# Gating and summing the output projection's weights: from the gate stages to a background task of the projection stream

## The chip, the cores and the metric

The kernel runs on one core of a Trainium2 chip. The metric is device time in microseconds (us) of one execution; lower is better. The core's engines are PE (TensorE, matrix products), DVE (VectorE), ACT (ScalarE), POOL (GpSimd) and SP (SyncE, which here only issues DMA loads). Each engine works through its own list of instructions in order, and waits where an instruction needs something that another engine or a DMA has not delivered.

## The reference, cut to what matters

One layer of a trunk whose two mixers (HGRN2 and GLA) share one input projection; sequence length and width are both 1024, everything is float32.

```python
mod = c_act @ ada_w + ada_b
shift, scale, gate = jnp.split(mod, 3, axis=-1)
h = rms_norm(x, norm_w) * (1.0 + scale) + shift
hq, hf, hi, hz, gq, gk, gv, gz, ga, mg = jnp.split(h @ w_in, IN_OFFSETS, axis=-1)
y_h = hgrn2_branch(hq, hf, hi, hz, ...)
y_g = gla_branch(gq, gk, gv, gz, ga, ...)
u_h, u_g = y_h @ w_branch[0], y_g @ w_branch[1]
mg = sigmoid(mg.reshape(B, T, 2, D_MODEL))
merged = mg[:, :, 0] * u_h + mg[:, :, 1] * u_g
x = x + gate[:, None, :] * (merged @ w_out)
return rms_norm(x, final_norm_w)
```

The factor `gate` scales columns, so `gate * (merged @ w_out)` is `merged @ (w_out * gate)`. The kernel multiplies the weights by the gate once. That multiplication, and the sums of blocks of the result, are what the change moves.

## The kernel before, in words

Every large product is done in float32 accuracy by splitting each operand into a rounded part `hi` (a cast on ACT, line L196 or L1285) and the rest `lo` (a subtraction on DVE, L197 or L1286), and by three PE products of the parts. On the time axis of the profile the kernel has these parts:

* The start (to about 75 us): modulation vectors, norm of the input, transposes.
* **The projection stream** (to about 806 us). Class `Stream` holds a list of jobs, one per block of columns of `w_in`; each job loads its weights (`load_feat`, L523, on SP), splits them and runs its PE products (L541). After each unit of a job, `weave` (L895) lets two tracks go on: `side`, which holds the attention of the heads (scores L683 to L781, outputs L848 and L850, squares and writes of the results through L1095, L1107 and L916), and `back`, a first-in first-out queue of background tasks. `back` holds first `prepare()` (factors of h and sums of other weights, `weight_sums`), and then `gate_side()`, which is appended when the first HGRN value block is done and makes the tile `gate_b`, the gate broadcast over the partitions (about 616 to 646 us).
* **Four seven-product stages** (`last_stages`): two gate stages b=0 (about 806 to 893 us) and b=1 (to about 975), which project the merge gates, and two branch stages b=2, 3 (to about 1130). Each is a two-by-two block product by seven products p in the order 1, 2, 5, 3, 6, 7, 4, with four pairs i of output tiles each. `Pair.run` holds the PE products (L1343); a pair's accumulator is turned into gates by ACT (L1414) and written to DRAM by POOL (L1415). Inputs are loaded ahead: factors by `fetch_factor` (L1230) and split by `build` (ACT L1263, DVE L1264, for p = 3 ACT L1260, DVE L1261), weights by `load_duo` (sums of weights L1274, plain ones L1278) and split by `prep_duo` (ACT L1285, DVE L1286). ACT copies of accumulators by `seed` and `snap_of` are L1323 and L1315.
* The output stage b=4 (1130 to 1210 us), again seven products, with the weights that the change is about: they are loaded back from DRAM by `load_w4` and split.

The first products of stage b=0 begin before the attention of the last head (h = 7) is done, so from about 795 to 860 us the last attention and the first gate products run interleaved. The bank of PSUM that the stage uses is lent to it when the last projection blocks have been read (`L953` on DVE multiplies the last one out of PSUM) and when the scores are done.

**The weights of the output projection** are four blocks for each of kk = 0, 1. In before, `load_wy(kk)` loads four 512 KB tiles (L1466, SP), `gate_wy` multiplies each by `gate_b` (L1474, DVE), `sum_wy` forms four sums of them (L1484, DVE), and `keep_wy` writes seven results per kk to DRAM (L1469, on POOL's queue, destination `wo`). These steps hang on hooks of the gate stages: `after(b, p, i, f)` puts f behind pair i of product p of stage b. For kk = 0 the load is at (0, 3, 0), the gating at (0, 6), the sums at (0, 7), and the tiles are freed at (1, 1, 0); for kk = 1 they are at (1, 1, 2), (1, 5), (1, 6) and (1, 7, 3). The multiplications and sums are held at that place of DVE's list by `tc.keep_in_program_order`; other instructions of an engine may be put in another order by a scheduler, by when it reckons their inputs and buffers to be ready.

All tiles of 4 KB per partition come from one pool `S`. A new tile takes the place of an older one, and whatever writes it must wait until the last reader of the older one is done; that reader can be a DMA write.

Of the kernel before, what the change touches and what calls it, by code (L numbers as in the profile page):

```python
# [9 lines left out]
F32 = mybir.dt.float32  # L10
# [5 lines left out]
P = 128  # L16
D = 1024
T = 1024
# [13 lines left out]
OUT_PRODUCTS = (1, 5, 3, 6, 7, 2, 4)  # L32
# [51 lines left out]
def hybrid_trunk_kernel(  # L84
# [6 lines left out]
    nc = tc.nc  # L91
# [5 lines left out]
    dp = ctx.enter_context(tc.tile_pool(name="dram", bufs=1, space=bass.MemoryType.DRAM))  # L97
# [3 lines left out]
    S = Slots(sp, N_SLOTS)  # L101
# [806 lines left out]
    stream = Stream()  # L908
# [5 lines left out]
    def put_act(acts, d, y):  # L914
        for half in range(2):
            nc.gpsimd.dma_start(acts[half][d // 2][:, d % 2 * 512:d % 2 * 512 + 512], y[:, half * 512:half * 512 + 512])  # L916
        S.free(y)
# [92 lines left out]
    def start_side(gen, wait=1):  # L1010
        stream.side.append([gen, wait])
# [30 lines left out]
    gate_b = [None]  # L1042

    def gate_side():

        gacc, gbias = S.get([D]), S.get([D])
        nc.sync.dma_start(gbias[0:1, :], ada_b[0:1, 2 * D:3 * D])
        for k in range(KT):
            b = S.get([D])
            nc.sync.dma_start(b, ada_w[0, k * P:(k + 1) * P, 2 * D:3 * D])  # L1050
            if k == 0:
                nc.vector.tensor_scalar_mul(gacc, b, cs[:, 0:1])
            else:
# [32 lines left out]
    def hgrn_attention(h):  # L1086
        st = h_state
        y = [None]
        sq = [None]

        def post(vh, half, po):
            if half == 0:
                y[0], sq[0] = st.pop(("z", h)), S.get([T])
            sl = slice(half * 512, half * 512 + 512)
            nc.scalar.activation(sq[0][:, sl], po, AF.Square)  # L1095
            nc.vector.scalar_tensor_tensor(y[0][:, sl], po, vec[:, R_HN + h:R_HN + h + 1],
                                           y[0][:, sl], ALU.mult, ALU.mult)

        yield from attention(st.pop(("q", h)), st.pop(("k", h)), st.pop(("f", h)), lambda: st[("v", h // 4)],
                             h % 4 * P, P, post, 4 if h % 4 == 1 else 3)  # L1100
        if h % 4 == 3:
            S.free(*st.pop(("v", h // 4)))
        put_act(yh_d, h, y[0])
        if ssq[0] is None:
            ssq[0] = sq[0]
        else:
            nc.gpsimd.tensor_add(ssq[0], ssq[0], sq[0])  # L1107
            S.free(sq[0])
        if h == 7:
            yield 2  # L1110
            rst = S.get([T])
            yield from inverse_root(rst, ssq[0], D)
            S.free(ssq[0])
            rst_h[0] = rst

    def hgrn_v(h):
        def done(v):
            h_state[("v", h // 4)] = v
            if h == 0:
# [59 lines left out]
    sources += [[branch(n, d) for d in range(0, 8, 2)] for n in (1, 0)]  # L1179

    w_sums = [[[dp.tile([P, T], F32, name=f"ws{b}{j}{i}") for i in range(4)] for j in range(2)] for b in range(4)]

    def weight_sums(b, i):
# [22 lines left out]
    def prepare():  # L1206
        yield from factors(h_d, f_x)
        for b in range(4):
            for i in range(4):
                yield from weight_sums(b, i)  # L1210

    stream.back.append([prepare(), 60])


# [4 lines left out]
    X_OF = {1: (0, 0), 2: (1, 0), 4: (1, 1)}  # L1219
# [50 lines left out]
    def load_duo(b, p, j):  # L1270
# [4 lines left out]
        else:  # L1275
            kh, f = X_OF[p]
            for a in range(2):
# [29 lines left out]
    class Pair:  # L1307
# [42 lines left out]
        def after(self, p):  # L1350
            bank, snap, out = self.bank, self.snap, outs[self.b]
            if p == 1:
                if self.b:
                    self.seed()
                else:
                    snap[1] = self.snap_of("a", -1.0)
            elif p == 2:
                out(2 * self.i, 0, bank["a"], False)
                R.free(bank.pop("a"))
            elif p == 5:  # L1360
                snap[5] = self.snap_of("e")
# [88 lines left out]
    for g in BUILT[1:]:  # L1450
        n = GROUPS.index(g)
# [3 lines left out]
    for d in range(8):  # L1455
        after(*((2, 5) if d % 2 else (1, 4)), d // 2, lambda d=d: load_gate1(d))

    w4_d = {p: [dp.tile([P, T], F32, name=f"wo{p}{kk}") for kk in range(2)] for p in OUT_PRODUCTS}
    w_rows = w_out[0].rearrange("(i two p) c -> two p i c", two=2, p=P)
    wy, w4_raw, W4 = {}, {}, {}  # L1460

    def load_wy(kk):
        for kh in range(2):
            for f in range(2):
                t = wy[kh, f] = S.get([2, 512])
                nc.sync.dma_start(t, w_rows[kh][:, 2 * kk:2 * kk + 2, f * 512:f * 512 + 512])  # L1466

    def keep_wy(p, kk, kh, f):
        nc.gpsimd.dma_start(w4_d[p][kk], wy[kh, f].rearrange("p a f -> p (a f)"))  # L1469

    def gate_wy(kk, n):
        kh, f = ((0, 0), (0, 1), (1, 0), (1, 1))[n]
        t = wy[kh, f]
        tc.keep_in_program_order(nc.vector.tensor_mul(  # L1474
            t, t, gate_b[0][:, f * 512:f * 512 + 512].unsqueeze(1).to_broadcast([P, 2, 512])))
        for p, at_ in X_OF.items():
            if at_ == (kh, f):
                keep_wy(p, kk, kh, f)
        if kk == 1 and n == 3:
            S.free(gate_b[0])  # L1480

    def sum_wy(kk, n):
        p, dst, other = ((7, (0, 0), (0, 1)), (5, (0, 1), (1, 1)), (6, (1, 1), (0, 0)), (3, (1, 0), (1, 1)))[n]
        tc.keep_in_program_order(nc.vector.tensor_add(wy[dst], wy[dst], wy[other]))  # L1484
        keep_wy(p, kk, *dst)

    def drop_wy():
        S.free(*wy.values())
        wy.clear()

    def load_w4(p):
        w4_raw[p] = [S.get([2, 512]) for _ in range(2)]
# [84 lines left out]
    def out_stage():  # L1577
        for p in OUT_PRODUCTS:
# [6 lines left out]
                S.free(*z)  # L1585
            for z in W4.pop(p):
                S.free(*z)

    for kk, (lead, first, then) in enumerate((((0, 3, 0), (0, 6), (0, 7)), ((1, 1, 2), (1, 5), (1, 6)))):
        after(*lead, lambda kk=kk: load_wy(kk))  # L1590
        after(*((1, 1, 0) if kk == 0 else (1, 7, 3)), drop_wy)
        for n in range(4):
            after(*first, n, lambda kk=kk, n=n: gate_wy(kk, n))
            after(*then, n, lambda kk=kk, n=n: sum_wy(kk, n))

    def last_of_11():
        combine(4, "22", "22", "11")
# [121 lines left out]
```

## Time and profile before

| what | value |
|---|---|
| time before, median of 3 runs | 1215.93 us (1215.64 to 1216.92) |
| the profiled execution's own time | 1216.46 us |
| its span in the profile | 1214.8 us |
| granted PE clock | 0.998 of full speed |
| busy: PE, DVE, ACT, POOL | 1184.1, 790.9, 546.9, 123.8 us |
| PE not busy within the span | 30.7 us |
| the operations that the change moves: DVE L1474 and L1484 | 8 x 1.22 us each |
| their loads (SP, L1466) and writes (POOL, L1469) | 8 and 14 of 512 KB |

A row of the timeline gives the start, the time an instruction (or a run of like ones) took, the engine, the line, the operation, "out<-in" by the names of tiles, the shapes, the count, and in brackets how long the engine sat idle just before and what ended that. Tile names without their number read `b` (pool tiles), `pd`, `pm`, `sc_ps` (PSUM). In the groups by line the columns behind the bar are busy time, mean ns of one, and idle time before. A row by windows gives the stretch, its length, the busy time of each engine with its count of instructions, the granted clock, the busy share of the DMA engines and the data rate.

### The profile page before, as it was taken

Reading aid. Unit: us, or ns where it says so; the run is one execution under the profiler, and the core shown is the slowest. Engines: PE = TensorE matmul, PEld = TensorE weight load, DVE = VectorE, ACT = ScalarE, POOL = GpSimd, SP = SyncE. Lnnn points to the kernel's source line nnn. Section 1 sums busy time; section 2 is a strip of 40 time slices with the busy share of each in tenths; the row PEclk is TensorE's granted clock in tenths of the full one; section 3 lists DMA queues with packets and bytes.
Section 4 is the critical chain, followed back from the end, with each engine's and each line's share of the span. In section 5 each row is a group of like instructions: output and inputs, shape, how many; then the busy total and the mean of one; then the engine's idle time right before and its main releaser. Section 6 shows DMA issues by size and latency. Waiting matters only on the chain.

```text
span 1214.8 us, 20860 instructions
## 1 busy us (share of the span) xinstructions
PE 1184.1 (97%) x8579; PEld 982.6 (81%) x8579; DVE 790.9 (65%) x1245; ACT 546.9 (45%) x797; POOL 123.8 (10%) x215
## 2 busy tenths in 40 slices
PE   5999999999999999999999999999999999999997
PEld 3777889889798888888887888877778888878886
DVE  4637444774848456877884365794653775988994
ACT  5646732434434244344332324455743544444554
POOL 4100000202111121121110101011220000000000
PEclk9999999999999999999999999999999999999999
DMA  9814000844444267255341112054697746435523
GB/s 320 277 70 139 18 19 19 293 141 161 156 152 149 66 207 249 94 179 169 108 174 47 59 53 70 36 174 158 227 343 277 260 160 208 135 104 173 174 104 122
DMA packets 130961, 183.51 MB, mean 151 GB/s; under 512 B 7467, under 2 KB 97633, under 8 KB 130866
## 3 DMA queue, kind: packets, MB, share of 16 engines
q1 hardware_dynamic: 117250, 136.87, 35.7%
q0 software_dynamic: 13568, 45.31, 9.6%
q8 instruction: 67, 1.10, 0.4%
q14 instruction: 28, 0.23, 0.1%
q10 hardware_dynamic: 48, 0.01, 0.0%
HBM read 132.87 MB, written 49.28 MB: 150 GB/s over the span
## 4 chain that ended last, share of the span: by engine, by line
PE 61%; issue 23%; DVE 3%; ACT 3%; POOL 2%; DMA 1%; POOLq 0%; ACTq 0%; DVEq 0%
PE pd L541 19%; PE pd L1343 9%; PE sc_ps L1343 5%; PE pm L1343 5%; PE pd L1520 3%; PE pd L643 2%; PE pd L644 2%; PE pd L645 2%; PE sc_ps L1520 2%; PE pm L848 1%; PE pd L352 1%; PE pm L829 1%; PE pm L850 1%; PE pm L1520 1%; PE sc_ps L352 1%
## 5 line engine op out<-in xcount | busy, mean ns | idle before, releaser
L541 PE MATMUL pd<-b,b 128*128 128x512 f32 x1632 | 387.4, 394 | 0.0
L541 PEld LDWEIGHTS pd<-b,b 128*128 128x128 f32 x1632 | 302.4, 188 | 64.8 <-issue 1.4
L1343 PE MATMUL pd<-b,b 128*128 128x512 f32 x720 | 173.7, 392 | 4.3 <-ACT b L1414 2.1
L1343 PEld LDWEIGHTS pd<-b,b 128*128 128x128 f32 x720 | 133.7, 188 | 35.7 <-ACT b L1414 3.2
L197 DVE TENSOR_TENSOR b<-b,b 128x1024 fp32r<-128x1024 f32 (+2 forms) x89 | 98.9, 1122 | 83.1 <-ACT b L196 65.4
L196 ACT CAST b<-b 128x1024 fp32r<-128x1024 f32 (+2 forms) x89 | 82.9, 948 | 92.1 <-DVE b L1199 14.6
L1286 DVE TENSOR_TENSOR b<-b,b 128x1024 fp32r<-128x1024 f32 x56 | 68.3, 1224 | 66.9 <-ACT b L1285 52.3
L1285 ACT CAST b<-b 128x1024 fp32r<-128x1024 f32 x56 | 58.3, 1050 | 73.9 <-PE pd L1343 20.6
L1343 PE MATMUL sc_ps<-b,b 128*128 128x512 f32 x324 | 79.4, 391 | 1.0 <-ACT scT L793 1.0
L600 PE MATMUL pd<-b,b 128*128 128x256 f32 x256 | 74.2, 290 | 0.0
L1264 DVE TENSOR_TENSOR b<-b,b 128x1024 fp32r<-128x1024 f32 x48 | 59.2, 1251 | 20.8 <-ACT b L1263 15.1
L602 PE MATMUL pd<-b,b 128*128 128x256 f32 x256 | 72.5, 283 | 0.0
L601 PE MATMUL pd<-b,b 128*128 128x256 f32 x256 | 72.4, 283 | 0.0
L1343 PEld LDWEIGHTS sc_ps<-b,b 128*128 128x128 f32 x324 | 60.3, 188 | 14.6 <-ACT scT L793 1.4
L1343 PE MATMUL pm<-b,b 128*128 128x512 f32 x300 | 72.1, 389 | 0.0
L1263 ACT CAST b<-b 128x1024 fp32r<-128x1024 f32 x48 | 49.9, 1050 | 41.2 <-PE pd L1343 16.0
L1343 PEld LDWEIGHTS pm<-b,b 128*128 128x128 f32 x300 | 56.3, 188 | 11.7
L352 PE MATMUL pd<-b,b 128*128 128x512 f32 x192 | 53.3, 410 | 2.0 <-ACT b L196 0.9
L1201 POOL DMA_DIRECT2D ws<-b x64 | 34.6, 541 | 192.0 <-DVE b L1195 86.5
L735 ACT COPY xb<-b 128x512 f32<-128x512 f32 x48 | 29.4, 620 | 49.4 <-PE sc_ps L715 26.7
L643 PE MATMUL pd<-b,b 128*128 128x512 f32 x128 | 51.3, 401 | 0.0
L644 PE MATMUL pd<-b,b 128*128 128x512 f32 x128 | 50.0, 390 | 0.0
(285 smaller groups left out, 1964.3 us busy)
## 6 DMA issues: line engine op xcount, KB each, us to landing
b<-in_w_in_dram SPq DMA_DIRECT2D x66, 512.0 KB, 4.2
ws<-b POOLq DMA_DIRECT2D x64, 256.0 KB, 3.3
b<-ws SPq DMA_DIRECT2D x32, 512.0 KB, 4.9
b<-in_x_dram SPq DMA_DIRECT2D x16, 512.0 KB, 5.7
b<-in_ada_w_dram SPq DMA_DIRECT2D x32, 256.0 KB, 6.9
b<-in_w_branch_dram SPq DMA_DIRECT2D x16, 512.0 KB, 4.4
b<-h SPq DMA_DIRECT2D x14, 512.0 KB, 4.3
wo<-b POOLq DMA_DIRECT2D x14, 512.0 KB, 5.7
```

Of the source, the lines that this page charges most:

```text
L196: nc.scalar.copy(hi, src)
L197: nc.vector.tensor_sub(lo, src, hi.bitcast(F32))
L352: nc.tensor.matmul(accs[f], wg(a, d, f), b[d][:, half * 512:half * 512 + 512], start=(d == 0 and n == 0), stop=(d == KT - 1 and n == 2))
L541: nc.tensor.matmul(ps[0:w, th * 512:(th + 1) * 512], a[:, k, 0:w], b[:, th * 512:(th + 1) * 512], start=(k == 0 and n == 0), stop=(k == KT ...
L600: nc.tensor.matmul(o, lh, hi[:, k % 4, :], start=(k == 0), stop=False)
L601: nc.tensor.matmul(o, lh, lo[:, k % 4, :], start=False, stop=False)
L602: nc.tensor.matmul(o, ll, hi[:, k % 4, :], start=False, stop=(k == KT - 1))
L643: nc.tensor.matmul(o, lh, hi[:, k % 2, :], start=(k == 0), stop=False)
L644: nc.tensor.matmul(o, lh, lo[:, k % 2, :], start=False, stop=False)
L1286: nc.vector.tensor_sub(lo, t, hi.bitcast(F32))
L1343: nc.tensor.matmul(o, a[:, sl], c, start=(p in (1, 5) and kt == 0 and n == 0), stop=(kt == 3 and n == 2), skip_group_check=True)
L1520: nc.tensor.matmul(o, a, b, start=(p in (1, 5) and kt == 0 and n == 0), stop=(kt == 3 and n == 2), skip_group_check=True)
```

## The change

The four steps leave the hooks and become a generator `out_weights()`, appended to the queue `back` right behind `gate_side()`. It waits until 12 tiles are free, loads one kk, gates the four tiles, sums them, frees them, and does the same for the other kk. `drop_wy` is folded in, the two `tc.keep_in_program_order` are dropped, and some names are defined earlier. `load_wy`, `keep_wy`, `gate_wy` and `sum_wy` are otherwise unchanged. In after, the load is line L1222, the write L1225, the gating L1230, the sum L1239, and the lines of before behind them are moved down by 45 (`fetch_factor` is L1275, `load_duo` L1319 and L1323, `prep_duo` L1330 and L1331, `build` L1305 to L1309, the ACT copy of `snap_of` L1360).

```diff
             h_state[("v", h // 4)] = v
             if h == 0:
                 stream.back.append([gate_side(), 4])
+                stream.back.append([out_weights(), 4])
...
+    def gate_wy(kk, n):
+        kh, f = ((0, 0), (0, 1), (1, 0), (1, 1))[n]
+        t = wy[kh, f]
+        nc.vector.tensor_mul(t, t, gate_b[0][:, f * 512:f * 512 + 512].unsqueeze(1).to_broadcast([P, 2, 512]))
...
+    def out_weights():
+        for kk in range(2):
+            while len(S.free_list) < 12:
+                yield 1
+            load_wy(kk)
+            yield 8
+            for n in range(4):
+                gate_wy(kk, n)
+                yield 2
+            yield 4
+            for n in range(4):
+                sum_wy(kk, n)
+                yield 3
+            S.free(*wy.values())
+            wy.clear()
...
-        tc.keep_in_program_order(nc.vector.tensor_mul(
-            t, t, gate_b[0][:, f * 512:f * 512 + 512].unsqueeze(1).to_broadcast([P, 2, 512])))
...
-        tc.keep_in_program_order(nc.vector.tensor_add(wy[dst], wy[dst], wy[other]))
...
-    for kk, (lead, first, then) in enumerate((((0, 3, 0), (0, 6), (0, 7)), ((1, 1, 2), (1, 5), (1, 6)))):
-        after(*lead, lambda kk=kk: load_wy(kk))
-        after(*((1, 1, 0) if kk == 0 else (1, 7, 3)), drop_wy)
-        for n in range(4):
-            after(*first, n, lambda kk=kk, n=n: gate_wy(kk, n))
-            after(*then, n, lambda kk=kk, n=n: sum_wy(kk, n))
```

The number of instructions on each engine stays the same. All 16 multiplications and sums, all 8 loads and all 14 writes now stand in the lists between the jobs of the projection stream that ran from about 640 to 715 us in before. Three places of the lists matter below.

SP's list where the stream loads the weights of its last jobs (L523, from `w_in`), before. `h_116` to `h_119` are the first factors of the gate stage, `b_6828` receives the weights of the job that runs at about 718 us:

```order
L523 DMA b_6233<-in_w_in_dram 128x8x128
L523 DMA b_6390<-in_w_in_dram 128x8x128
L523 DMA b_6828<-in_w_in_dram 128x8x128
L523 DMA b_6473<-in_w_in_dram 128x8x128
L523 DMA b_6535<-in_w_in_dram 128x8x128
L523 DMA b_6645<-in_w_in_dram 128x8x128
```

SP's list at the same job in after, where those weights go into `b_6859`:

```order
L1222 DMA b_6677<-in_w_out_dram 128x2x512
L1222 DMA b_6679<-in_w_out_dram 128x2x512
L1222 DMA b_6683<-in_w_out_dram 128x2x512
L1222 DMA b_6681<-in_w_out_dram 128x2x512
L1275 DMA b_7220<-h_116 128x1024
L1275 DMA b_7446<-h_118 128x1024
L523 DMA b_6859<-in_w_in_dram 128x8x128
L1275 DMA b_7447<-h_119 128x1024
```

The load stood third among the stream's loads and now stands behind the four loads of kk = 1 and two loads of factors. The tile `b_7446` ahead of it takes the place of the tile `b_6679`, so that its load waits for the write of `b_6679` to DRAM (`wo_772<-b_6679` in POOL's list).

DVE's list from the masks of the last head's scores to the operation (L720) behind which its last score products wait, before:

```order
L953 TENSOR_TENSOR b_7437<-b_7437,pd_7336 128x1024
L690 TENSOR_TENSOR blk<-sc_ps,eye_679 128x256
...
L698 COPY_PREDICATED blk<-mask_683,sc_ps 128x64
L1286 TENSOR_TENSOR b_7529<-b_7408,b_7528 128x1024
L717 TENSOR_TENSOR b_7164<-xb,tot_726 128x64x12
L718 TENSOR_TENSOR tot_726<-tot_726 128x64
L719 TENSOR_TENSOR tot_726<-tot_726 128x64
L721 TENSOR_TENSOR tot_726<-tot_726 128x64
L746 TENSOR_TENSOR tot_726<-tot_726 128x32
...
L720 TENSOR_TENSOR b_7330<-b_7330,tot_726 128x64x12
```

The same stretch of DVE's list in after:

```order
L953 TENSOR_TENSOR b_7483<-b_7483,pd_7382 128x1024
L1309 TENSOR_TENSOR b_7689<-b_7649,b_7687 128x1024
L690 TENSOR_TENSOR blk<-sc_ps,eye_679 128x256
...
L698 COPY_PREDICATED blk<-mask_683,sc_ps 128x64
L717 TENSOR_TENSOR b_7210<-xb,tot_726 128x64x12
L718 TENSOR_TENSOR tot_726<-tot_726 128x64
L1331 TENSOR_TENSOR b_7781<-b_7578,b_7780 128x1024
L719 TENSOR_TENSOR tot_726<-tot_726 128x64
L1306 SCALAR_TENSOR_TENSOR b_7871<-b_7801,b_7869 128x1024
L721 TENSOR_TENSOR tot_726<-tot_726 128x64
L1331 TENSOR_TENSOR b_7850<-b_7670,b_7849 128x1024
L720 TENSOR_TENSOR b_7376<-b_7376,tot_726 128x64x12
```

Between L953 and L720 stood one operation of 128x1024 that belongs to the gate stage (L1286), and now there are four (L1309, L1331, L1306, L1331); rows that are the same on both sides (L695 to L711, two more L746) are left out here. The three L746 moved behind L720.

ACT's list at about 850 us, where the last head's outputs are squared (L1095), the accumulators copied (L1315, in after L1360) and the sum of squares cast (L196), before:

```order
L1095 ACTIVATE b_7845<-pm_7848 128x512
L1315 COPY b_7821<-sc_ps 128x512
L1263 CAST b_7940<-b_7889 128x1024
L1315 COPY b_7887<-pd_7440 128x512
L196 CAST b_7906<-b_4458 128x1024
```

And in after:

```order
L1095 ACTIVATE b_7891<-pm_7894 128x512
L1330 CAST b_8010<-b_7916 128x1024
L1360 COPY b_7867<-sc_ps 128x512
L196 CAST b_7952<-b_4458 128x1024
L1308 CAST b_7986<-b_7935 128x1024
L1360 COPY b_7933<-pd_7486 128x512
```

The copy out of `pd` stood ahead of the cast L196, which reads the sum that POOL makes (L1107), and now stands behind it.

More of the change, by code (lines that the diff above doesn't have):

```diff
@@ L1179, in hybrid_trunk_kernel @@
     sources += [[branch(n, d) for d in range(0, 8, 2)] for n in (1, 0)]
+    X_OF = {1: (0, 0), 2: (1, 0), 4: (1, 1)}
     w_sums = [[[dp.tile([P, T], F32, name=f"ws{b}{j}{i}") for i in range(4)] for j in range(2)] for b in range(4)]
@@ L1210, in prepare, with load_wy, keep_wy, sum_wy @@
                 yield from weight_sums(b, i)
+    w4_d = {p: [dp.tile([P, T], F32, name=f"wo{p}{kk}") for kk in range(2)] for p in OUT_PRODUCTS}
+    w_rows = w_out[0].rearrange("(i two p) c -> two p i c", two=2, p=P)
+    wy = {}
+    def load_wy(kk):
+        for kh in range(2):
+            for f in range(2):
+                t = wy[kh, f] = S.get([2, 512])
+                nc.sync.dma_start(t, w_rows[kh][:, 2 * kk:2 * kk + 2, f * 512:f * 512 + 512])
+    def keep_wy(p, kk, kh, f):
+        nc.gpsimd.dma_start(w4_d[p][kk], wy[kh, f].rearrange("p a f -> p (a f)"))
+    def gate_wy(kk, n):
+        kh, f = ((0, 0), (0, 1), (1, 0), (1, 1))[n]
+        t = wy[kh, f]
+        nc.vector.tensor_mul(t, t, gate_b[0][:, f * 512:f * 512 + 512].unsqueeze(1).to_broadcast([P, 2, 512]))
+        for p, at_ in X_OF.items():
+            if at_ == (kh, f):
+                keep_wy(p, kk, kh, f)
+        if kk == 1 and n == 3:
+            S.free(gate_b[0])
+    def sum_wy(kk, n):
+        p, dst, other = ((7, (0, 0), (0, 1)), (5, (0, 1), (1, 1)), (6, (1, 1), (0, 0)), (3, (1, 0), (1, 1)))[n]
+        nc.vector.tensor_add(wy[dst], wy[dst], wy[other])
+        keep_wy(p, kk, *dst)
+    def out_weights():
[13 more added lines that the diff above has]
+            wy.clear()
     stream.back.append([prepare(), 60])
@@ L1218, in hybrid_trunk_kernel @@
     BUILT = [g for g in GROUPS if g[0] != 1]
-    X_OF = {1: (0, 0), 2: (1, 0), 4: (1, 1)}
     BANK = {1: "a", 2: "a", 5: "e", 3: "e", 6: "b", 7: "b", 4: "b"}
@@ L1456, in hybrid_trunk_kernel @@
         after(*((2, 5) if d % 2 else (1, 4)), d // 2, lambda d=d: load_gate1(d))
[L1458 to L1474, printed above, removed]
-            t, t, gate_b[0][:, f * 512:f * 512 + 512].unsqueeze(1).to_broadcast([P, 2, 512])))
[L1476 to L1483, printed above, removed]
-        tc.keep_in_program_order(nc.vector.tensor_add(wy[dst], wy[dst], wy[other]))
[L1485 to L1489, printed above, removed]
+    w4_raw, W4 = {}, {}
     def load_w4(p):
```

## The prediction

> **What bounds the kernel now.** I read the windows first, then PE's waits, then the timeline around each wait. The windows give the busy time of each engine in the parts that the change touches, PE, PE's weight loads, DVE, ACT and POOL from the left.
>
> ```profile
> 640.00:720.00 80.00, 80.00 (x648) 64.12 (x647) 32.73 (x60) 24.80 (x38) 3.44 (x3) 1.00 0.18 50
> 795.00:860.00 65.00, 61.99 (x521) 49.88 (x521) 45.41 (x70) 36.41 (x56) 9.53 (x10) 1.00 0.58 199
> 860.00:900.00 40.00, 38.18 (x167) 31.05 (x168) 26.41 (x27) 24.47 (x32) 9.68 (x18) 1.00 0.76 265
> 900.00:970.00 70.00, 70.00 (x310) 57.98 (x309) 35.56 (x34) 31.63 (x43) 4.27 (x8) 1.00 0.83 279
> ```
>
> PE is never idle where the work goes to (640 to 720 us), nor in the second gate stage, which it leaves (900 to 970), although the DMAs are busy there for 0.83 of the time. It is idle for 3.01 us between 795 and 860 and for 1.82 us between 860 and 900. What the change can win lies in these 4.8 us; what it can lose is open. PE's waits name them:
>
> ```profile
> PE pd L1343 <- ACT b L1414: 2.1, 2, 1.8
> PE pd L1343 <- DVE b L953: 1.5, 1, 1.5
> PE sc_ps L1343 <- ACT scT L793: 1.0, 1, 1.0
> PE pd L1343 <- ACT b L1315: 0.2, 1, 0.2
> ```
>
> So 10 us of moved DVE work in each gate stage is not 10 us on the path: the path is PE, and PE waits at five places there, for 4.7 us.
>
> **The moved work itself.** Of 30 moved instructions the sixteen on DVE cost
>
> ```profile
> L1474 DVE TENSOR_TENSOR b<-b,b 128x1024 f32<-128x1024 f32 x8 | 9.7, 1220 | 0.5 <-DMA b<-in_w_out_dram 0.5
> ```
>
> for the gating, and the sums, of the same shape, as much: 8 x 1.22 = 9.8 us for each kk. These rows show where they can go:
>
> ```profile
> 645.19 1.23 DVE L197 TENSOR_TENSOR b<-b,b 128x1024 fp32r<-128x1024 f32 x1 [6.22 <-ACT b L196]
> 655.77 0.69 DVE L710 TENSOR_TENSOR xb<-b,tot 128x512 f32<-128x512 f32 x1 [9.35 <-PE sc_ps L683]
> 700.02 1.22 DVE L953 TENSOR_TENSOR b<-b,pd 128x1024 f32<-128x1024 f32 x1 [1.48 <-ACT b L952]
> 709.84 1.03 ACT L1077 ACTIVATE b<-pd 128x1024 f32<-128x1024 f32 x1 [7.51 <-PE pd L541]
> 710.90 0.82 DVE L1079 TENSOR_SCALAR b<-b,oml,lb 128x1024 f32<-128x1024 f32 x1 [9.66 <-ACT b L1077]
> ```
>
> The kk = 0 half fills the 9.35 us of idle time ahead of 655.77, the kk = 1 half the 9.66 us ahead of 710.90. Some of it overhangs by a microsecond; the weights that the stream splits there (L197) are read 20 us later. L953, which empties a PSUM bank, moves from 700 to about 705 us behind the last gating; PE takes that bank for its next job about 709.8 us, when the job ahead is done and ACT starts to read it (709.84). **I take 0** for this work; without that cover it would be 10 us per half.
>
> **Term a, SP's queue.** The moved list puts a load that PE needs behind a load that waits for a write. Its rows are the load, the split of what it brings, and the product that needs DVE's list up to L679:
>
> ```profile
> 646.45 0.37 SPq L523 DMA_DIRECT2D b<-in_w_in_dram  x1
> 694.76 0.55 POOL L916 DMA_DIRECT2D yh<-b  x1
> 711.67 1.05 ACT L196 CAST b<-b 128x1024 fp32r<-128x1024 f32 x1
> 715.57 1.21 DVE L197 TENSOR_TENSOR b<-b,b 128x1024 fp32r<-128x1024 f32 x1
> 716.70 0.64 DVE L679 TENSOR_TENSOR xb<-xb,b 128x256 f32<-128x256 f32 x1
> 717.89 1.31 PE L683 MATMUL sc_ps<-xb,b 128*32 128x80 f32 x64
> ```
>
> In before the load went out at 646.45 and had 61 us to spare. In after it stands behind `b_7446<-h_118`, which waits until `b_6679` is gated (row at about 702 to 705 us, since the fourth load can go out only when the write of 694.76 has left its tile, about 697), summed (about 706 to 708) and written. How long writes and loads of 512 KB take, from issue to landing, first for `wo` in the crowded gate stage, then for POOL's writes of `h` at a quiet time, then for the stream's loads from 636 to 740 us:
>
> ```profile
> DMA to landing us min/median/max: 4.0/5.7/7.6
> DMA to landing us min/median/max: 2.9/3.1/6.6
> DMA to landing us min/median/max: 3.7/3.8/3.8
> ```
>
> The DMAs are busy 0.18 here, so I take the quiet rows: write out at 707, landed at 710.3 (709.6 to 713), the load out at 710.8, landed at 714.8 (713.6 to 717.3). ACT's cast (1.05) brings it to 715.9, against the 715.57 at which L197 could start; L679 then ends at 717.7 and PE, which comes free at 717.9, loses little. **I take +0.4** (0 to +3.4; the upper end with 5.5 us for the write and 5 for the load).
>
> The Trainium skill, page "DMA: Bandwidth & Descriptors", section "Anatomy of one DMA — SWDGE (gpsimd) path", fits such a DMA by 2.0 us plus the bytes over 436 GB/s, an estimate of 3.2 us for 512 KB; no row of `wo` here comes below 4.0. By it this term would be about 0.
>
> **Term b, the crossover at 810 to 836 us.**
>
> ```profile
> 809.48 1.23 DVE L1264 TENSOR_TENSOR b<-b,b 128x1024 fp32r<-128x1024 f32 x1
> 810.62 1.23 DVE L953 TENSOR_TENSOR b<-b,pd 128x1024 f32<-128x1024 f32 x1
> 811.90 5.73 PE L1343 MATMUL pd<-b,b 128*128 128x512 f32 x24 [1.49 <-DVE b L953]
> 817.93 0.60 DVE L746 TENSOR_TENSOR tot<-tot 128x32 f32<-128x32 f32 x3
> 818.52 0.96 DVE L720 TENSOR_TENSOR b<-b,tot 128x768 f32<-128x768 f32 x1
> 822.62 0.19 DVE L759 COPY_PREDICATED blk<-mask,sc_ps 128x32 f32<-128x32 int32 x1
> 824.04 0.63 PE L770 MATMUL sc_ps<-xb 128*16 128x16 f32 x56
> 834.02 1.89 PE L1343 MATMUL sc_ps<-b,b 128*128 128x512 f32 x7 [0.96 <-ACT scT L793]
> ```
>
> DVE starts one operation right behind the other in these rows, so what the scheduler puts ahead is paid in full. Ahead of L953 stand the same six splits as before, but in other places, and beside the addition that POOL makes for each head (L1107). What such a meeting costs DVE shows one head earlier:
>
> ```profile
> 752.00 2.40 POOL L1107 TENSOR_TENSOR b<-b,b 128x1024 f32<-128x1024 f32 x1 [0.31 <-ACT b L1095]
> 753.27 2.21 DVE L197 TENSOR_TENSOR b<-b,b 128x1024 fp32r<-128x1024 f32 x1 [0.63 <-ACT b L196]
> ```
>
> L197 takes 2.21 there and 1.21 in the row at 715.57: 1.0 more. I allow L953 that +1.0 (-0.5 to +2.2: a meeting that before had goes, or a second comes).
>
> The Trainium skill, page "SBUF — State Buffer", section "Who interferes with whom", says that a DVE instruction with two inputs in SBUF contends with a GpSimd instruction that reads SBUF, and that whoever issues first keeps the shared pair while the other is blocked for the whole instruction. The row agrees that DVE is held, but for 1.0 and not for all of POOL's 2.40; a full block of a split that starts right behind POOL would make L953 some 2.4 late, and the sum 1.4 higher.
>
> Behind L953 three more operations of 128x1024 come before L720. They start about 1.14 us apart (809.48 and 810.62), so 3 x 1.14 = 3.4, less 0.6 for the three L746 that move behind L720. L759 ends 1.2 us before PE's L770 (822.81 and 824.04): 2.8 - 1.2 = 1.6 that PE would lose, and 2.6 with the delay of L953. The operations that went ahead are gone from the stretch behind, where DVE's way to L793 gets shorter, so the waits of 0.96 and of 0.3 (the L1414 row's 2.1 less its longest), together 1.2, should go: 2.6 - 1.2 = **+1.4** (-0.5 to +3.2).
>
> **Term c, ACT at 850 us.**
>
> ```profile
> 850.46 0.58 ACT L1315 COPY b<-pd 128x512 f32<-128x512 f32 x1
> 852.22 1.05 ACT L196 CAST b<-b 128x1024 fp32r<-128x1024 f32 x1 [1.18 <-POOL b L1107]
> 859.83 2.56 PE L1343 MATMUL pd<-b,b 128*128 128x512 f32 x10 [0.15 <-ACT b L1315]
> ```
>
> The copy out of `pd` ended at 851.04 and now comes behind a cast that waits for POOL until 852.2. Behind it stand further casts and the second copy, for which PE waits at 859.83. A delay of about 1.35 there, less what is slack, gives **+1.2** (0 to +2.1).
>
> **Term d, the end of stage b = 0.**
>
> ```profile
> 887.31 0.54 POOL L1415 DMA_DIRECT2D gate<-b  x1 [3.01 <-ACT b L1414]
> 887.84 0.54 POOL L1469 DMA_DIRECT2D wo<-b  x1
> 892.22 0.60 ACT L1414 ACTIVATE b<-pd 128x512 f32<-128x512 f32 x1 [0.76 <-DMA gate<-b]
> 892.87 1.43 PE L1343 MATMUL pd<-b,b 128*128 128x512 f32 x5 [1.82 <-ACT b L1414]
> ```
>
> PE waits 1.82 for a gate, which waits 0.76 for a tile that the write of 887.31 holds; seven writes of `wo` share queue and DMAs with it, and the casts ahead on ACT wait for loads in the same crowd. With those gone most of it goes: **-1.5** (-1.8 to 0). Stage b = 1 gives nothing, since PE has no idle time there.
>
> **Sum:** 0 + 0.4 + 1.4 + 1.2 - 1.5 = +1.5. The profiled execution took 1216.46, so 1218.0; it lies 0.53 above the median of the runs, so the median comes to **1217.4**.
>
> **The rivals.** A measurement of this kernel can tell about 0.2% from no change, 2.4 us: below 1213.5 is faster, above 1218.4 slower.
>
> *Slower: SP's queue at full price.* If the weights of `b_6859` land after about 715.2, all that is later is paid at L683. For: the fourth load waits for the write of 694.76, and `wo` writes took 5.7 in the middle. Against: the DMAs are quiet. With +2.9 in place of 0.4 the median is 1219.9.
>
> *Faster: the crossover costs nothing.* If the splits that move ahead fill waits of DVE (for data that comes later in after), b and c are 0 and only d is left, at its full 1.8: 1216.46 - 1.8 - 0.53 = 1214.1. For: as many operations stand ahead of L953 as before. Against: none of the DVE rows from 809 to 823 shows idle time ahead of it. It would be below 1213.5 only if the 1.49 at 811.9 went too (1212.6).
>
> *The change doesn't do what it says in the gate stage.* If PE's 1.82 at 892.87 come from the casts of weights (L1285) ahead on ACT and not from the crowd, d is 0: 1218.9.
>
> **How the numbers follow.** Forecast 0.46, of which a quarter lies above 1218.4; slower rival 0.26; faster 0.18, of which a third lies below 1213.5; no change in the gate stage 0.10. Faster is then 0.06 and some for what I overlook, 0.08; slower 0.11 + 0.24 + 0.07 = 0.42; the rest, 0.50, within 0.2%. The range leaves out the ends: from 1213.9 (the faster rival with a little over) to 1221.5 (the slower rival with the upper half of b).
>
> **What would show it.** In the profile after: no idle PE from 640 to 715 us; the start of L683 near 717.9 to 718.3 (term a, 720 or more for the slower rival); PE's idle time ahead of L770 at 824 (b, 1 to 3 us); the wait for L1315's line at 860 (c, over 1 us); and no wait of 1.8 us at 893 (d). The forecast is wrong if the stream shows a wait that these rows don't name, above all of PE for weights, or if DVE at the crossover is idle.

## The result, and the profile after

The changed kernel takes 1224.37 us (median of 6 runs, 1221.40 to 1226.50), against 1215.93 for the kernel before (6 runs, 1215.64 to 1217.28): a ratio of 1.0067, with a 95% interval from 1.0051 to 1.0082. Run again later beside other kernels it took 1222.08 (6 runs), a ratio of 1.0050 (1.0035 to 1.0064). It is slower by 6 to 8 us, where 1.5 was forecast, and it lies above the range. The profiled execution took 1225.01 us (span 1223.1).

The windows of the changed kernel, with the columns as in the prediction:

```profile
640.00:720.00 80.00, 77.44 (x622) 62.57 (x625) 49.32 (x74) 23.44 (x36) 10.92 (x17) 0.99 0.56 185
795.00:860.00 65.00, 57.93 (x510) 46.74 (x509) 47.83 (x72) 34.26 (x54) 9.11 (x10) 1.00 0.51 170
860.00:900.00 40.00, 38.01 (x167) 30.76 (x165) 17.71 (x19) 25.63 (x32) 3.78 (x7) 1.00 0.49 153
```

The moved work is where it was expected: DVE is busy for 49 us instead of 33 between 640 and 720, and the gate stages have lost it. But PE is now idle for 2.56 us in the stream, for 7.1 instead of 3.0 between 795 and 860, and still for 2.0 between 860 and 900. Its waits after 600 us name the places:

```profile
PE pd L1388 <- DVE b L953: 3.3, 1, 3.3
PE sc_ps L683 <- DVE xb L679: 2.6, 1, 2.6
PE sc_ps L1388 <- ACT scT L793: 1.3, 1, 1.3
PE pd L1388 <- ACT b L1360: 1.2, 1, 1.2
PE pd L1388 <- ACT b L1459: 1.1, 2, 0.8
PE pd L1388 <- DVE b L1375: 1.1, 1, 1.1
PE pd L1388 <- ACT b L1362: 0.9, 1, 0.9
PE sc_ps L770 <- DVE blk L759: 0.6, 1, 0.6
```

How far the same PE product (counted in order within its line) lies behind its time in before gives the price of each place. This execution ran 1.73 us ahead in the stream, up to 719 us; 1.6 us of that lead is there from the stream's first products on, far ahead of the moved work:

| product | start before | start after | shift | what lies between |
|---|---|---|---|---|
| L541, up to 719 us | 517.59 | 515.86 | -1.73 | |
| first gate product (L1343, L1388) | 806.06 | 808.57 | +2.51 | wait at L683 and slow clock, +4.24 |
| L1343 after the crossover | 847.35 | 853.46 | +6.11 | waits for L953, L759, L743, L793, +3.60 |
| behind ACT's copy at 850 | 859.83 | 866.75 | +6.93 | wait for L1360, +0.8 |
| at 880 | 880.00 | 889.14 | +9.14 | waits for L1362 and L1375, +2.2 |
| end of stage 0 | 892.87 | 901.15 | +8.28 | wait for L1459 smaller than L1414's was, -0.9 |
| output stage (L1520, in after L1534) | 1130.35 | 1138.61 | +8.26 | nothing |

**The wait at L683.** SP's, POOL's, DVE's and PE's rows around 715 us, then the windows of that stretch:

```profile
708.55 0.34 SPq L1275 DMA_DIRECT2D b<-h  x1
708.98 0.54 SPq L523 DMA_DIRECT2D b<-in_w_in_dram  x1
```

```profile
704.38 0.53 POOL L1225 DMA_DIRECT2D wo<-b  x1 [2.87 <-DVE b L1239]
```

```profile
716.87 1.23 DVE L197 TENSOR_TENSOR b<-b,b 128x1024 fp32r<-128x1024 f32 x1 [2.96 <-ACT b L196]
718.01 0.63 DVE L679 TENSOR_TENSOR xb<-xb,b 128x256 f32<-128x256 f32 x1
```

```profile
718.79 2.07 PE L683 MATMUL sc_ps<-xb,b 128*32 128x80 f32 x64 [2.56 <-DVE xb L679]
```

```profile
713.00:716.00 3.00, 3.00 (x15) 2.34 (x13) 0.91 (x2) 0.21 (x1) 0.00 (x0) 1.00 0.92 267
716.00:719.00 3.00, 0.44 (x15) 0.24 (x17) 2.13 (x3) 0.84 (x1) 0.00 (x0) 1.00 0.29 117
719.00:722.50 3.50, 3.50 (x68) 2.99 (x60) 3.36 (x7) 0.93 (x2) 0.00 (x0) 0.52 0.00 0
```

The chain is the one of term a: the write of 704.38 lands, the factor load of 708.55 may go, and the weights go out right behind it at 708.98. They went out when I had reckoned (710.8, less the 1.7 us by which this execution runs ahead), but took longer: DVE's split waits for the cast, of 1.05 us, until 716.87, so that the weights landed about 715.8, nearly 7 us after their issue and not 4 (in the second profile, shown below, the cast starts 6.2 us after the issue). The DMAs are busy at 0.92 here, not at 0.18. Then comes what no term had: from 719.0 to 722.5 the granted clock is 0.52, so that 3.5 us of products do the work of 1.8. The wait of 2.56 costs 4.24 in all.

**The crossover.** DVE, POOL, ACT and PE from 800 us, and for comparison ACT's rows up to L952 in before (those at 807.42 and 808.38):

```profile
800.38 3.67 DVE L1331 TENSOR_TENSOR b<-b,b 128x1024 fp32r<-128x1024 f32 x1
803.98 0.74 DVE L1096 SCALAR_TENSOR_TENSOR b<-pm,vec,b 128x512 f32<-128x512 f32 x1
```

```profile
800.56 2.40 POOL L1107 TENSOR_TENSOR b<-b,b 128x1024 f32<-128x1024 f32 x1
805.01 0.55 POOL L916 DMA_DIRECT2D yh<-b  x1 [2.05 <-DVE b L1096]
```

```profile
810.46 2.00 ACT L1308 CAST b<-b 128x1024 fp32r<-128x1024 f32 x2 [5.46 <-DMA yh<-b]
813.32 1.00 ACT L952 ACTIVATE b<-pd 128x1024 f32<-128x1024 f32 x1
```

```profile
807.42 1.05 ACT L1285 CAST b<-b 128x1024 fp32r<-128x1024 f32 x1
808.38 1.01 ACT L952 ACTIVATE b<-pd 128x1024 f32<-128x1024 f32 x1
```

```profile
811.53 2.36 DVE L1309 TENSOR_TENSOR b<-b,b 128x1024 fp32r<-128x1024 f32 x2 [1.00 <-ACT b L1308]
814.95 1.22 DVE L953 TENSOR_TENSOR b<-b,pd 128x1024 f32<-128x1024 f32 x1
```

```profile
816.21 0.96 PE L1388 MATMUL pd<-b,b 128*128 128x512 f32 x3 [3.30 <-DVE b L953]
```

The split L1331, which the scheduler put ahead of the second L1096, took 3.67 us beside POOL's addition, so L1096 ended late, POOL's write of `yh` went out at 805.01, and the cast L1308 on ACT, whose tile that write held, stood idle for 5.46 us. L952, which feeds L953, stood behind it; in before L952 was done at 809.4, behind casts that had no such wait. On DVE L953 came last too, behind the splits of the late casts, for which DVE was idle for 1.00 us. L1096 didn't need the split, and neither L952 nor L953 needed the casts; they stood in one list.

The second execution profiled, of the run repeated later, shows what of this repeats. Its waits, and DVE and POOL at 800 us:

```profile
PE pd L1388 <- DVE b L953: 1.8, 1, 1.8
PE pd L1388 <- ACT b L1459: 1.7, 2, 1.4
PE sc_ps L683 <- DVE xb L679: 1.4, 1, 1.4
PE pd L1388 <- ACT b L1360: 1.2, 1, 1.2
```

```profile
799.61 1.21 DVE L1331 TENSOR_TENSOR b<-b,b 128x1024 fp32r<-128x1024 f32 x1
801.41 2.19 DVE L679 TENSOR_TENSOR xb<-xb,b 128x256 f32<-128x256 f32 x1
```

```profile
799.79 3.29 POOL L1107 TENSOR_TENSOR b<-b,b 128x1024 f32<-128x1024 f32 x1
```

```profile
813.00:816.00 3.00, 2.06 (x6) 1.62 (x7) 3.00 (x4) 2.24 (x4) 0.00 (x0) 0.74 0.00 0
816.00:819.50 3.50, 3.50 (x13) 2.81 (x12) 3.50 (x10) 0.00 (x0) 0.00 (x0) 0.74 0.44 150
```

The same waits are there, smaller: here the split took 1.21 and POOL's addition was drawn out (3.29 instead of 2.40), and with it DVE's L679 (2.19, where it takes 0.63 in the first profile). Why it went the other way round the rows don't show: DVE's split starts 0.18 us ahead of POOL's addition in both profiles. The low clock is there too, but about the wait for L953 (0.74 in both windows, partly while PE waits) and not behind L683.

### The profile page after: what moved, and what is told of

Read it like the earlier page. It is cut to its first block, busy times and chain, and to the rows that moved or that the text cites. A ratio compares the mean times of both kernels' runs of the same rounds, so it can differ in the third digit from the quotient of the medians.

```text
span 1223.1 us, 20856 instructions
## 1 busy us (share of the span) xinstructions
PE 1186.1 (97%) x8579; PEld 983.9 (80%) x8579; DVE 791.9 (65%) x1245; ACT 547.3 (45%) x797; POOL 123.6 (10%) x215
## 4 chain that ended last, share of the span: by engine, by line
PE 60%; issue 22%; DVE 3%; DMA 3%; ACT 3%; POOL 2%; SPq 0%; POOLq 0%; ACTq 0%; DVEq 0%
PE pd L541 17%; PE pd L1388 10%; PE sc_ps L1388 5%; PE pm L1388 5%; PE pd L1534 3%; PE pd L643 2%; PE pd L644 2%; PE pd L645 2%; DMA b<-in_w_in_dram 2%; PE sc_ps L1534 2%; PE pm L848 2%; PE pm L829 1%; PE pm L850 1%; PE pd L352 1%; PE pm L1534 1%
## 5 line engine op out<-in xcount | busy, mean ns | idle before, releaser
L541 PE MATMUL pd<-b,b 128*128 128x512 f32 x1632 | 388.5, 394 | 0.0
L541 PEld LDWEIGHTS pd<-b,b 128*128 128x128 f32 x1632 | 303.0, 188 | 65.4 <-issue 1.7
L1388 PE MATMUL pd<-b,b 128*128 128x512 f32 x720 | 173.8, 392 | 8.1 <-DVE b L953 3.3
L1388 PEld LDWEIGHTS pd<-b,b 128*128 128x128 f32 x720 | 133.8, 188 | 39.9 <-DVE b L953 3.7
L196 ACT CAST b<-b 128x1024 fp32r<-128x1024 f32 (+2 forms) x89 | 82.9, 947 | 108.5 <-PE pd L541 20.0
L1331 DVE TENSOR_TENSOR b<-b,b 128x1024 fp32r<-128x1024 f32 x56 | 72.3, 1293 | 70.5 <-ACT b L1330 41.7
L1330 ACT CAST b<-b 128x1024 fp32r<-128x1024 f32 x56 | 58.3, 1048 | 63.9 <-PE pd L1388 18.0
L1388 PE MATMUL sc_ps<-b,b 128*128 128x512 f32 x324 | 79.4, 391 | 1.3 <-ACT scT L793 1.3
L1388 PEld LDWEIGHTS sc_ps<-b,b 128*128 128x128 f32 x324 | 60.3, 188 | 14.6 <-ACT scT L793 1.7
L1388 PE MATMUL pm<-b,b 128*128 128x512 f32 x300 | 72.1, 389 | 0.0
L1308 ACT CAST b<-b 128x1024 fp32r<-128x1024 f32 x48 | 49.7, 1048 | 46.6 <-PE pd L1388 15.9
L1309 DVE TENSOR_TENSOR b<-b,b 128x1024 fp32r<-128x1024 f32 x48 | 57.7, 1224 | 19.9 <-ACT b L1308 12.7
L1388 PEld LDWEIGHTS pm<-b,b 128*128 128x128 f32 x300 | 56.3, 188 | 11.7
```

What stands on the lines that cost most here:

```text
L196: nc.scalar.copy(hi, src)
L541: nc.tensor.matmul(ps[0:w, th * 512:(th + 1) * 512], a[:, k, 0:w], b[:, th * 512:(th + 1) * 512], start=(k == 0 and n == 0), stop=(k == KT ...
L1331: nc.vector.tensor_sub(lo, t, hi.bitcast(F32))
L1388: nc.tensor.matmul(o, a[:, sl], c, start=(p in (1, 5) and kt == 0 and n == 0), stop=(kt == 3 and n == 2), skip_group_check=True)
```

## The experiments

The theory after the result: the moved work itself costs nothing; the loss is in the order in which the scheduler put other instructions (SP's loads before 720 us, the splits and casts at 800 to 815), and in the low clock that follows long waits of PE. Its rival: the moved work crowds the stream, in whatever order. In the diffs the names are those of the changed kernel.

### The factor loads held back

```diff
-            nc.sync.dma_start(raw_f[g][kk], f_x[p][kk])
+            ld = nc.sync.dma_start(raw_f[g][kk], f_x[p][kk])
+            if b == 0 and p in (1, 2):
+                tc.keep_in_program_order(ld)
```

> The changed kernel, with the loads of the gate stage's first factors (products 1 and 2) held behind the loads that the program issues before them, so that the weights of the job at 718 us no longer stand behind them in SP's list; DVE's and ACT's lists at the crossover stay as in the changed kernel. Theory 1 (the loss comes from where other instructions ended up): PE's wait of 2.6 us at L683 and the stretch of low granted clock behind it (about 1.7 us) both go, some 4.3 us, to about 1220 (1219 to 1221). Theory 2 (the moved work crowds the stream, in whatever order): the load still lands late among the seven writes, DMAs 0.8 busy, and the time stays at 1223 to 1225.

Measured: 1220.68 us (6 runs, 1218.17 to 1223.67), ratio 1.0042 (1.0027 to 1.0056). The waits of its profile that matter:

```profile
PE pd L1390 <- DVE b L953: 2.2, 1, 2.2
...
PE sc_ps L683 <- DVE xb L679: 0.8, 1, 0.8
```

The wait at 718 us is gone (0.14 there; the 0.8 is one job later, at 761). The time came down to where the first theory put it, though against the repeated run it is only 1.4 lower. The low clock did not go: the mean granted clock of its runs is 0.9963, and its profile has a stretch of half clock at 812 to 815 us, behind the wait for L953. The order on SP is a part of the loss, the smaller one.

### The multiplications and sums held in program order again

```diff
-        nc.vector.tensor_add(wy[dst], wy[dst], wy[other])
+        tc.keep_in_program_order(nc.vector.tensor_add(wy[dst], wy[dst], wy[other]))
```

(and the multiplication likewise)

> The changed kernel with the two calls that hold the multiplications and sums in program order put back, as they were before the change. SP's list then has the weights of the job at 718 us ahead of the factors, DVE's list from L953 to L720 stays as in the changed kernel. Theory 1: no wait at L683 and no low clock behind it, the wait for L953 (3.3 us) stays, about 1220. Theory 2 (crowding): no change, 1223 to 1225.

Measured: 1223.39 us (5 runs, 1221.57 to 1225.59), ratio 1.0065 (1.0053 to 1.0078). The expectation of the first theory missed. The wait at L683 is gone, as it said, but others have come:

```profile
780.60 0.66 PE L770 MATMUL sc_ps<-xb 128*16 128x16 f32 x62 [1.37 <-DVE blk L759]
782.24 0.69 PE L781 MATMUL sc_ps<-b,b 128*64 128x64 f32 x16 [0.66 <-DVE b L743]
789.98 1.83 PE L829 MATMUL pm<-b,b 128*128 128x128 f32 x14 [0.58 <-ACT b L808]
```

Three of the held sums now stand later in DVE's list, at 768.18, 770.75 and 774.00 (L1240), among the score operations of a head, and so does a split (L1332 at 777.46). So an order at that place can cost 2.6 us as well, and the calls that the change dropped were not what was missing.

### One half only

The first run leaves kk = 1 on the hooks of the second gate stage, the other leaves kk = 0 on those of the first:

```diff
-        for kk in range(2):
+        for kk in (0,):
             while len(S.free_list) < 12:
```

> Only kk = 0 in the background of the stream; kk = 1 stays on its hooks in the second gate stage. SP's order of the stream's last loads and factors and DVE's and ACT's lists at the crossover are then as in before. Theory 1: the first half costs nothing in the stream, and the first gate stage loses its wait of 1.8 us at 893 in part: 1214 to 1216. Theory 2 (the moved work crowds the stream): half of the loss, about 1220.

> Only kk = 1 in the background of the stream (at the place where kk = 0 is in the changed kernel); kk = 0 stays on its hooks in the first gate stage. Half of the moved work, like the run with the first half, but the first gate stage keeps its writes and sums. Theory of term d (the wait of 1.8 us at 893 belongs to these writes and sums): it comes back, and the time is 1 to 2 us above the run with the first half, 1216 to 1217.5. Rival (that wait belongs to the casts of weights or to chance): the same time as the run with the first half, 1215.5.

Measured: 1215.48 us (11 runs, 1212.83 to 1217.36), ratio 0.9991 (0.9982 to 1.0001), with the first half in the stream; 1216.65 (11 runs, 1215.40 to 1218.51), ratio 1.0004 (0.9995 to 1.0012), with the other. Half of the work in the stream costs nothing, which speaks against the crowd. In both, SP's order and the lists at 800 us are those of before, and so is the wait for L953 (1.5). The first half's profile has no wait of 1.8 at 893 any more. With kk = 0 left in the first stage, the profile shows waits of 0.98 and 0.53 at 888, for the splits of weights, and the kernel lies 0.13% above the other half, some 1.6 us, though the two intervals overlap a little. Term d is about right in size, as far as that goes; that it hangs on the split of weights in one profile and on the gate's tile in the other shows that no single wait owns it.

### POOL's addition on DVE

```diff
-            nc.gpsimd.tensor_add(ssq[0], ssq[0], sq[0])
+            (nc.vector if h == 6 else nc.gpsimd).tensor_add(ssq[0], ssq[0], sq[0])
```

> The changed kernel, with POOL's addition L1107 of the head h = 6 done by DVE, so that no split runs beside a POOL addition at 800 us; SP's list at 718 us is as in the changed kernel, and DVE's and ACT's lists at the crossover nearly so. Theory 1a (POOL's addition holds the split L1331, which took 3.67 us, and all that is queued behind it up to L953): the split takes 1.2 us, the second L1096 ends about 1.2 us earlier (2.4 less 1.2 for the addition on DVE), PE's wait for L953 goes from 3.3 to about 2, and the median falls by about 1 us to 1223. Theory 1b (the wait is set by the order of the lists alone): the wait for L953 stays at 3.3 and the time at 1224.

Measured: 1220.72 us (5 runs, 1218.85 to 1221.69), ratio 1.0039 (1.0027 to 1.0051). The split takes 1.22 and the wait for L953 is 1.9, not 3.3:

```profile
PE pd L1388 <- DVE b L953: 1.9, 1, 1.9
```

The repeated run of the changed kernel had 1.8 there without this edit, so the meeting with POOL fits the difference of its two profiles, and is not the whole loss. The time fell below the 1223 of the theory that the wait bore out. It is 1.4 us below the repeated run; part of that can be the clock (mean 0.998 here, 0.997 there), and how much is left open.

### The order at the crossover, alone and with SP's

The splits of the gate stage's first factors (products 2 and 5; product 3 is named in the set, but `build` splits it in a branch without the call, so that it stays free) and five weight tiles are held, on ACT and on DVE, behind what the program issues before them:

```diff
-        nc.scalar.copy(hi, t)
-        nc.vector.tensor_sub(lo, t, hi.bitcast(F32))
+        cc, ss = nc.scalar.copy(hi, t), nc.vector.tensor_sub(lo, t, hi.bitcast(F32))
+        if duo in PINNED_DUOS:
+            tc.keep_in_program_order(cc)
+            tc.keep_in_program_order(ss)
```

(in `prep_duo`, and the same in `build`; L953 then stands right behind L701 in DVE's list)

> The changed kernel with only the splits held in program order (the order at the crossover as in the run with both orders), and SP's list left as in the changed kernel, so that the weights of the job at 718 us still stand behind the factor whose tile waits for a write. Theory 1 (two separate losses in the order): the wait at L683 of 1.5 to 2.6 us comes back, with or without a stretch of half clock behind it (1.7 us), and the wait for L953 stays away: 1217 to 1220. Rival (the loads alone make no loss when the crossover has slack): 1215.5 as with both orders.

> The changed kernel with the factor loads held back as in the run with the held loads, and the splits of the gate stage's first factors and weights held in program order, so that L953 stands right behind L701 in DVE's list and no split or factor cast stands ahead of L952 on ACT. Theory 1 (order): the wait for L953 at 812 us (2.2 to 3.3 us) goes too; what is left of the loss are the waits of about 1.2, 1.0 and 0.8 behind 850 us: 1217.5 to 1219. Rival (the splits come too late for PE instead): waits for L1330 or L1331 take its place, 1220 to 1222.

Measured, with SP's list left as in the changed kernel: 1217.37 us (12 runs, 1215.41 to 1222.39), ratio 1.0014 (1.0003 to 1.0025). With the factor loads held as well: 1215.51 (11 runs, 1214.27 to 1216.75), ratio 0.9996 (0.9988 to 1.0005). The waits of the first, then of the second:

```profile
PE sc_ps L683 <- DVE xb L679: 1.8, 1, 1.8
```

```profile
PE pd L1395 <- ACT b L1466: 1.3, 1, 1.3
PE sc_ps L683 <- DVE xb L679: 1.0, 1, 1.0
PE pd L1395 <- DVE b L1382: 1.0, 1, 1.0
PE pd L1395 <- ACT b L1367: 0.6, 1, 0.6
```

No wait for L953 is left in either. The second is faster than its theory had it (1217.5 to 1219). With both orders mended, all 16 operations, 8 loads and 14 writes stand in the stream and the kernel is as fast as before, and as the kernel before with the same splits held (1215.84, below): the whole loss was order. The wait for L683 that is left in it is one job later, at 761. The four kernels make a square:

| ratio to before | SP's list as changed | factor loads held |
|---|---|---|
| lists at the crossover as changed | 1.0067 and 1.0050 | 1.0042 |
| splits held at the crossover | 1.0014 | 0.9996 |

SP's order is worth 1 to 3 us, the crossover 4 to 6. The second is more than the wait for L953 in any profile (1.8 to 3.3), for two reasons. From the first gate product to the one after the crossover (as in the table of shifts) the changed kernel loses 3.60 us against before in its first profile, 2.33 in its second and 1.93 with the loads held; in the last two this holds a stretch of half clock, which costs 1.7. With the splits held the same way is 1.60 and 2.10 shorter than in before, mostly because the wait of 1.5 that before itself has for L953 is gone too. The mean granted clock over the runs points the same way: 0.9963 with the loads held alone, 0.9983 with both.

### The changed kernel again

> The changed kernel itself once more, beside the others on one chip, for the size of its loss and for what repeats in its profile. Theory 1: the waits at L683 (1.5 to 2.6) and for L953 (about 3) are there again, and half clock shows in some runs, not always at the same place; 1222 to 1226. Rival (the half clock behind L683 belongs to that wait): it is at 719 us again.

Measured: 1222.08 us (6 runs, 1219.80 to 1225.12), ratio 1.0050 (1.0035 to 1.0064). Both waits are there again, the one for L953 smaller than expected (1.8), and the low clock was not at 719: the first theory. The profile is shown with the result.

### The order at the crossover without the move, and with the first half

> The kernel before with the same splits held in program order and nothing moved. Theory 1: its wait of 1.5 us for L953 at 812 goes and nothing else changes: 1214.5 to 1215.5. Rival (the splits come too late): 1217 or more.

> The first half in the background and the same splits held in program order. Theory 1: the gains of the first half (1.8 at 893) and of the order (1.5 at 812) add up: 1213 to 1214.5. Rival (one wait takes the place of the other): 1215.5 as with the first half alone.

> The first half in the background, and fewer splits held (the factors of product 2 and three weight tiles), so that ACT's copies of accumulators stand ahead of the cast L196 at 850 us as in before. Theory 1: without the wait of 3.6 us that the longer list of held splits made at 852, the gains of 1.5 at 812 and 1.8 at 893 add up: 1213 to 1214.5, faster than both kernels. Rival: another wait takes their place, 1215.5.

Measured: the kernel before with the splits held, 1215.84 us (11 runs, 1214.01 to 1217.42), ratio 0.9996 (0.9987 to 1.0005). Its wait for L953 is gone, but the time hardly moves, and lies just above what the first theory gave (1214.5 to 1215.5): by the shifts of the profile it gains 1.7 us at the crossover and gives 1.3 back by 860. The first half with all splits held, 1216.50 (12 runs, 1212.90 to 1218.95), ratio 1.0000 (0.9990 to 1.0010): the rival. One wait is left, and it is long:

```profile
852.18 4.36 PE L1397 MATMUL pd<-b,b 128*128 128x512 f32 x12 [3.56 <-ACT b L1369]
```

```profile
852.20:855.00 2.80, 2.80 (x9) 2.26 (x10) 0.89 (x1) 2.77 (x3) 0.00 (x0) 0.74 0.04 18
855.00:858.50 3.50, 3.50 (x13) 2.75 (x12) 1.51 (x2) 1.89 (x3) 0.00 (x0) 0.72 0.66 198
```

ACT's copy of an accumulator (L1369) stood behind the cast L196, which waited for POOL's addition: term c's place, at three times its size, and half clock for a time behind it.

With fewer splits held (the factors of product 2 and three weight tiles), that copy stands ahead of the cast, and the kernel takes **1213.72 us** (12 runs, 1212.46 to 1214.83), ratio 0.9978 (0.9969 to 0.9987): faster than both kernels. Its longest waits:

```profile
PE pd L1397 <- ACT b L1468: 0.9, 2, 0.6
```

So most of the two gains that the prediction saw in the gate stages (1.8 at 893, 1.5 at 812) can be had, 2.5 us of 1216, by moving half of the work and keeping the order.

## Why the prediction was wrong

- **The moved work itself: 0, right.** Both orders mended, the full move costs nothing on balance (0.9996, and 0.9996 for the kernel before with the same splits held).
- **Term a, SP's queue: +0.4, too small.** The mechanism was right, down to the rows: the weights stood behind the factor load, which waited for the write. The step "the DMAs are busy 0.18 here, so I take the quiet rows" failed: 0.18 was the share in before, without the writes and loads that the change brings there. It was 0.92, and the weights took 6.8 us instead of 4. The wait was 2.56 in one profile and 1.41 in the other, and 1.9 us of time between the two kernels that differ in this alone with the crossover mended. That is near the rival that I gave 0.26 to, but the time is above the 1219.9 of that rival too, because term b failed as well.
- **Term b, the crossover: +1.4 (-0.5 to +3.2), the step that failed most.** The prediction counted operations between L953 and L720, and reckoned that PE would lose 1.6 to 2.6 at L770; it waited 0.60 there in one profile and not at all in the other. The wait came ahead of L953: not through the number of splits, which is six in both, but through ACT's list, where a cast that waited for a tile stood ahead of L952, a row that I had not looked at. DVE was idle behind that cast, which the prediction had named as a sign against it. The waits of 0.96 and 0.3 "should go", and stayed (1.26 and 0.29). The places together cost +3.60 in the first profile and +2.33 in the second, and mending the order brought 4.7 to 5.2 us, 1.6 to 2.1 of it from the wait that before has there.
- **The lock beside POOL.** The first profile has L1331 at 3.67 beside an addition of 2.40, 2.45 more than alone. That is the full block that the Trainium skill, page "SBUF — State Buffer", section "Who interferes with whom", describes for the one of the two that issues second. The trace agrees in the length; which one issued first it doesn't show (0.18 us between the starts, DVE ahead, in both profiles). The sum of the prediction had 1.0 for such a meeting; the full block stood beside it.
- **Term c, ACT at 850: +1.2, about right.** The wait is 1.17 in both profiles of the changed kernel, against 0.15 in before. The shift over that stretch is +0.8.
- **Term d, the end of stage 0: -1.5, too large.** The wait there is 0.84 and 1.38 instead of 1.82, which is -1.0 and -0.4. With half of the work moved it is gone. Ahead of it lies something that the prediction lacked: waits of 0.9 and 1.1 at 877 and 889, +2.2 in the shift. ACT's rows of the first:

```profile
874.36 1.05 ACT L1308 CAST b<-b 128x1024 fp32r<-128x1024 f32 x1 [3.39 <-DMA b<-fx]
876.26 0.59 ACT L1362 ACTIVATE b<-pd 128x512 f32<-128x512 f32 x1
```

  A copy for which PE waits stands behind a cast that waits for a factor's load. This wait is in no other profile of a kernel with the whole move. The other one, at 889, is in all of them, at 0.9 to 1.1, also with both orders mended; there a split on DVE waits for a cast, and the cast for a tile that the write of a gate holds. What brings it was not tested.
- **The clock: no term at all.** Half clock for some 3.4 us costs 1.7 in the first profile of the changed kernel, and shows in the second one too. The Trainium skill, page "TensorE: Matmul & The Clock Gate", section "Part 1: The HAM clock gate (the "warmup" mystery)", says that the clock falls to half after an idle window of about 3.4 us whose place is not tied to the program. The length and the half agree with 719.0 to 722.5 at 0.52. That the place changes from run to run agrees too. The waits ahead of it were shorter here, 2.56 and 1.80, and the longest wait, 3.30 for L953 in the first profile, had no half clock behind it.

The range was too narrow because it treated each wait as costing its own length, and each list apart: a late write on POOL became a late cast on ACT, a late L953 on DVE, and a slow PE.

## What to carry to other kernels

When work is moved under a scheduler that places instructions by when tiles come free, its own cost is the small part: look in each in-order list for what now stands behind an instruction that waits for a tile, on every engine up to the one that the bound engine waits for. A share of busy DMAs or a transfer's time read from the stage before the move does not hold for it after the move. And a wait of PE of about 2 us or more can cost more than its length, through the clock.

## What the runs showed of the hardware that I had not expected

Half clock also comes without a wait. In the run with only the crossover mended PE is busy throughout, and the clock falls just after products that use one row of the array (L1063, "1*128": one row, 128 columns), at 640.7 and 642.8 us:

```profile
640.00:643.50 3.50, 3.50 (x8) 0.88 (x6) 1.03 (x1) 1.54 (x2) 0.00 (x0) 1.00 0.00 0
643.50:647.00 3.50, 3.50 (x9) 2.48 (x9) 3.50 (x4) 0.58 (x1) 0.42 (x1) 0.58 0.00 0
```

The profile with POOL's addition on DVE has the same at 645 us. That these products bring it is not shown: in the other profiles the clock stays full behind them. Each profile here has at most one such stretch ahead of the end. The mean granted clock over a kernel's runs followed the waits on the whole: 0.9975 to 0.9983 for before and for the kernels whose longest wait in the profile is at most 1.8 us, 0.9963 to 0.9970 for those with a wait of 2.0 to 3.6, with two out of line (POOL's addition on DVE, 0.998 with 1.9, and the changed kernel again, 0.997 with 1.8). One kernel's own times follow its clock as well: of 35 runs of before, from 1213.8 to 1220.3 us, the 9 at a granted clock of 0.997 have a median of 1217.2, the 21 at 0.998 one of 1215.8, the 3 at 0.999 one of 1214.9.
